# Query weight sums begun in the attention, MLP copies moved to w_xo's panels, a fourth raw buffer and two bank copies moved ahead on ScalarE

## The chip, the core and the metric

The kernel runs on one core of one Trainium2 chip. The metric is the device time of one execution in microseconds (us). Shorter is better. The engines are named as the profile names them: PE is TensorE, DVE is VectorE, ACT is ScalarE, POOL is GpSimd and SP is SyncE, which here only issues DMAs.

## The reference, cut to what matters

One layer of a streaming encoder: 512 tokens, width 1024, float32 in and out.

```python
hn = rmsnorm(h, norm_mix_g)
proj = hn @ w_in        # fox q,k,v,f | hgrn q,f,i,g
fox_out = fox_attention(...)         # 8 heads of 64, causal, forgetting bias
rec = hgrn2_chunkwise(...)           # 4 heads, state 128x128, gated recurrence
h = h + concat([fox_out, rec]) @ w_out
h = h + memory_cross_attention(rmsnorm(h, norm_x_g), mem_n, w_xq, w_xkv, w_xo)
u = rmsnorm(h, norm_ff_g) @ w1
h = h + square(relu(u)) @ w2
return rmsnorm(h, final_norm_g)

def memory_cross_attention(h, mem_n, w_q, w_kv, w_o):
    q = h @ w_q                      # 4 heads of 256; the queries of this text
    k, v = split(mem_n @ w_kv)
    p = softmax(q k^T / 16)
    return (p v) @ w_o
```

## The kernel before

**Arithmetic.** Every float32 product is made of three passes over tensors that are split into a rounded part (hi, "h") and a remainder (lo, "l"): hi x hi, hi x lo and lo x hi. A weight therefore passes through four steps: a DMA brings a raw block of 128 x 1024 values (0.5 MB) into a raw buffer, ACT copies it into a hi tile (line 189), DVE subtracts to get the lo tile (line 193), and PE uses both. Four hi and four lo tiles exist (`whp`, `wlp`), so a split waits until PE has left an earlier unit.

**Seven products for eight.** Several large products are done as 2 x 2 blocks with seven block products in the place of eight. Each needs combinations of blocks. Products are named 1 to 7; numbers 1, 2 and 3 take a weight block as it stands, 5, 7, 6 and 4 take sums of blocks. Part of the input projection, the queries (`w_xq`), the MLP's `w1` ("u", up) and `w2` ("d", down) are done in this way. For the queries there are two groups g = 0 and 1, hence 14 products, called 01, 11, 02 and so on in the order `QORDER`:

```python
QORDER = "01 11 02 05 06 07 04 03 15 12 16 17 14 13"
```

The sums over weight blocks are made in DRAM by DMAs. For each set (q, u or d, and a group) the function `sum_jobs` (line 535) first copies three blocks from DRAM to DRAM on SP's queue (line 542, "copies"; tiles `wsq`, `wsu`, `wsd`), and then POOL issues three accumulating DMAs on these copies (line 552, "sums"). There are 17 sets: two for the queries, seven for up, eight for down, so 51 copies and 51 sums. Sum number 4 of the queries and the MLP is made in SBUF: the raw tile of product 6 is kept, and POOL adds one more block to it (line 326) after the split for product 6 has read it. Product 4 then splits the same tile.

**When copies are issued.** The copies wait in the list `copies`. They are taken from it when weight panels are loaded (`load_unit`, line 199): each half panel takes as many as the table `COPIES` gives for the number of panels so far. Panel numbers: 12 to 18 are the last of w_in and first of the memory values, 19 and 20 the second memory values, 21 to 24 the memory keys, 25 to 28 w_out, 29 to 42 the 14 query units, 43 to 46 w_xo. Eight copies come earlier (`product_unit`). `q_unit` (line 302) takes one more for each query unit. The first loads of the MLP (`add_first`) take a copy each for four parts, and a sum whose copy has not been made by then fetches it.

**When sums are issued.** `Presum` (line 556) counts `spent`, the time of the matmuls that call `tick`, at 2400 columns per us. From the first value of the table `PACE` on, a sum is issued each time `spent` has grown by the gap that PACE gives for that stretch. The sum waits for the matmul at which it was due. Sets are taken in turn, two at a time: all six of the queries first, then u1 and d0, u2 and d1, and so on.

**Order around the change.** PE's order is written out by hand (`manual_schedule`): chunked recurrence, then 16 steps of attention with filler work between them (second value half, the third and fourth q/k pair, memory values, memory keys), then w_out (`residual`, "wo"), then the first seven query products back to back (`q_product`, line 1459, called for `QORDER[:7]`), then cross attention with the other seven as filler, w_xo ("xw"), and the MLP. ACT, DVE, POOL and SP are ordered by a list scheduler by priority, which is the order in the program, shifted by `ahead(n)`: positive n moves an instruction forward. Splits in `next_panel` have `PW` = -20. `P1` is 20. The order is fixed at build time, and each engine then runs in order. A tile pool hands out its buffers as that scheduler frees them.

**The query products.** Products of one group share PSUM banks U, V and Y. Product 1 fills U; V is started with a copy of U (line 1464) when product 2 comes; product 6 goes on in U, which is then copied to Y (line 1483); product 7 goes on in U after that copy has read it. Product 5 starts Y and its result is copied out (line 1481). The inputs 5, 6, 7 and 3 are sums of blocks of x (`x1_sums`, line 1413: DVE steps at line 1421, hi on ACT at 1425, lo on DVE at 1427 and 1429), written after the last residual sum of w_out (line 1362). Raw buffers of query units: two tiles of `wrp` and the one of `t4p` in turn, and for product 6 a tile of the pool `s4` (12 tiles), which also holds hT (4), the memory values (4) and the differences `xdif`, `xdif7`.

**w_xo and the MLP.** Raw buffers for w_xo come from `wrp` and `t4p`; the MLP has five in turn, and product 6 and the closing tiles come from `s4`.

Of the kernel before, what the change touches and what calls it, by code (L numbers as in the profile page):

```python
# [12 lines left out]
AF = mybir.ActivationFunctionType  # L13
# [6 lines left out]
D = 1024  # L20
# [12 lines left out]
P1, P2, P3, P4, PW = 20, 20, 20, 10, -20  # L33
# [6 lines left out]
NEG = -3.0e38  # L40
SEVEN = (1, 2, 3, 4, 5, 6, 7)
RAWS, HB, LOADS = 5, 4, 8
COPIES = {12: 2, 19: 1, 20: 0, 24: 1}
PACE = (150.0, 4.7), (301.0, 11.5)


@with_exitstack
def emit(
# [22 lines left out]
    te, ve, ac, gp = nc.tensor, nc.vector, nc.scalar, nc.gpsimd  # L71
# [26 lines left out]
    def s4(shape, name, dt=F32):  # L98
        return s4p.tile([P] + shape, dt, tag="s4", name=name)
# [7 lines left out]
    def t4(name):  # L107
        return t4p.tile([P, D], F32, tag="t4", name=name)

    def t2(name, dt=F32, shape=(S,)):  # L110
        return t2p.tile([P] + list(shape), dt, tag="t2", name=name)
# [6 lines left out]
    def mm(name, shape=(S,)):  # L118
        return mmp.tile([P] + list(shape), F32, tag="mm", name=name)
# [4 lines left out]
    def sc(name, shape=(S,)):  # L124
        return scp.tile([P] + list(shape), F32, tag="sc", name=name)
# [49 lines left out]
    state = {"used": 0, "halves": 0}  # L175
    copies, copied = deque(), set()
    UW, UK = WT + FH, KC // 2

    def new_parts(shape, name):
        pad = [P, UK * (UW + FH)]  # L180
        hi = whp.tile([P, shape[0] * shape[1]], R, tag="wh", name=f"wh{name}", padded_shape=pad)
        lo = wlp.tile([P, shape[0] * shape[1]], R, tag="wl", name=f"wl{name}", padded_shape=pad)
        return [t.rearrange("p (k n) -> p k n", k=shape[0]) for t in (hi, lo)]

    def split_of(hi, lo, raw):
        def split(what="hl"):
            at = None
            if "h" in what:
                at = ac.activation(hi, raw, AF.Copy)  # L189
            if "v" in what:  # L190
                ve.tensor_copy(hi, raw)
            if "l" in what:
                at_lo = ve.tensor_tensor(lo, raw, f(hi), ALU.subtract)  # L193
                return at or at_lo
            return at

        return split

    def load_unit(name, spec, ks, parts=1, between=None):
# [12 lines left out]
        for q in range(parts):  # L212
# [5 lines left out]
            if between is not None:  # L218
                between(q)
            for _ in range(next((n for at, n in reversed(COPIES.items()) if len(stream) >= at), 0)):  # L220
                if copies:
# [80 lines left out]
    def q_unit(g, name):  # L302
        hi, lo = new_parts([UK, WT], f"q{g}{name}")
        stream.append(([hi], [lo]))
        if name == "4":
            raw = q_raw.pop(g)
        else:
            if name == "6":
                raw = q_raw[g] = s4([UK, WT], f"wrq{g}{name}")
            else:  # L310
                state["halves"] += 1
                if state["halves"] % 3 == 0:
                    raw = t4(f"wrq{g}{name}")
                else:
                    raw = wrp.tile([P, D], F32, tag="wr", name=f"wrq{g}{name}", padded_shape=[P, UK * UW])
                raw = raw.rearrange("p (k n) -> p k n", k=UK)
            if name in SUMS:
                src = wsum["q", g, name]
            else:
                src = block_q(g, {"1": "00", "2": "10", "3": "11"}[name])  # L320
            nc.sync.dma_start(raw, src)
        if copies:
            tc.keep_in_program_order(copies.popleft()())
        jobs = [split_of(hi, lo, raw)]
        if name == "6":
            jobs.append(lambda: tc.keep_in_program_order(gp.dma_start(raw, block_q(g, "10"), accum_op=ALU.add)))
        return jobs
# [60 lines left out]
    def ahead(n):  # L388

        return tc.high_priority(offset=n) if n else nullcontext()  # L390

    class Fill:
        def __init__(self):
            self.q = deque()
            self.credit = 0.0
# [132 lines left out]
    def block_q(g, rc):  # L528
        r, c = int(rc[0]), int(rc[1])
        n0 = g * HG + c * WT  # L530
        return w_xq[r * S : (r + 1) * S, n0 : n0 + WT].rearrange("(k p) n -> p k n", p=P)
# [24 lines left out]
    class Presum:  # L556
        def __init__(self):
            self.jobs, self.spent, self.next, self.at = deque(), 0.0, PACE[0][0], None

        def emit(self):  # L560
            while self.jobs:
# [5 lines left out]
                tc.add_manual_dep(dma.ins, self.at.ins.name, sync, reason="presum")  # L567
                if self.spent >= PACE[-1][0]:
                    tc.keep_in_program_order(dma)
# [4 lines left out]
        def tick(self, us, at):  # L574
            self.spent, self.at = self.spent + us, at
            while self.jobs and self.spent >= self.next:
                gap = next(gap for begin, gap in reversed(PACE) if self.next >= begin)
                if gap is None:
                    self.next = min(begin for begin, _ in PACE if begin > self.next)
                    continue  # L580
# [205 lines left out]
    for hp in range(2):  # L786
# [8 lines left out]
        for j in range(2):  # L795
            h = 2 * hp + j
            ps = mm(f"gq{h}")
# [52 lines left out]
    U, W = [], []  # L850
# [112 lines left out]
    for li, m in enumerate(mlev):  # L963
# [10 lines left out]
        for hp in range(2):  # L974
# [3 lines left out]
            ps = sc(f"lv{hp}{m}", (NT, 2, w))  # L978
# [465 lines left out]
    qbank, y5s = {}, {}  # L1444
# [14 lines left out]
    def q_product(g, name):  # L1459
        b = {"5": "Y", "3": "Y", "2": "V"}.get(name, "U")  # L1460
        if (g, b) not in qbank:
            qbank[g, b] = (pvt if (g, b) == (0, "Y") else mm)(f"xq{b}{g}").rearrange("p (i n) -> p i n", i=2)
            if b == "V":
                ac.activation(qbank[g, b], qbank[g, "U"], AF.Copy)
        ps = qbank[g, b]
        (whi,), (wlo,) = next_panel()
        xh, xl = x1s[name]
        for k in range(UK):
            for i in range(2):
                ws, begin = slice(i * P, (i + 1) * P), name in "15" and k == 0 and i == 0  # L1470
                te.matmul(ps[:, i, :], whi[:, k, ws], xh[:, k, :], start=begin, stop=False, skip_group_check=True)
                te.matmul(ps[:, i, :], whi[:, k, ws], xl[:, k, :], start=False, stop=False, skip_group_check=True)
                at = te.matmul(ps[:, i, :], wlo[:, k, ws], xh[:, k, :], start=False, stop=k == UK - 1, skip_group_check=True)
            yield presum.tick(6 * WT / 2400, at)
        if name == "2":
            q_out(2 * g, 0, ps, 1.0)
        elif name == "4":
            q_out(2 * g, 1, ps, 1.0)
        elif name == "5":
            y5s[g] = t2(f"xy5{g}", F32, (2, M))  # L1480
            ac.activation(y5s[g], ps, AF.Copy)
        elif name == "6":
            ac.activation(qbank[g, "Y"], ps, AF.Copy)
        elif name in "73":
            t = t2(f"xt{name}{g}", F32, (2, M))
            ve.tensor_tensor(t, ps, y5s[g], ALU.add)
            q_out(2 * g + 1, 1 if name == "7" else 0, t, -1.0)

    for g, name in QORDER[:3]:
        run_now(q_product(g, name))  # L1490
# [4 lines left out]
    for g, name in QORDER[3:QN]:  # L1495
        run_now(q_product(g, name))
# [685 lines left out]
```

## Time and profile before

| | |
|---|---|
| median of 3 runs | 762.55 us (762.04 to 767.69) |
| the profiled execution | 764.74 us |
| its span, first to last instruction | 763.0 us |
| mean granted PE clock | 0.989 |
| PE busy | 742.7 us, 97% of the span |
| PE weight load (PEld) busy | 653.8 us, 86% |
| DVE busy | 585.3 us, 77% |
| ACT busy | 475.3 us, 62% |
| POOL busy | 221.2 us, 29% |
| moved by DMA | 168.68 MB |

The profile is of one execution. Its times start at the first instruction of the span; the 1.7 us between span and execution time lie around it. A row of a timeline gives start, duration, engine, line, operation, tile written and tiles read, and in brackets how long the engine was idle before and who released it. A row of the waits gives engine, tile and line that waited, then who it waited for, with us in total, times, and the longest. A row of a stage gives its length, busy us (with the number of instructions) of PE, PEld, DVE, ACT and POOL, the granted PE clock, the DMA share (mean busy share of the 16 DMA engines; it can pass 1 where packets overlap) and GB/s. A row of DMA issues gives tile and source, queue, count, size and median us from issue to landing. A matmul's duration is modelled with its pipeline; the distance between starts shows the rate.

### The profile page before, as it was taken

What the parts mean: (1) busy time and instruction counts of PE and PEld (TensorE: products, weight loads), DVE (VectorE), ACT (ScalarE), POOL (GpSimd) and SP (SyncE); (2) the same over time, 40 slices, a digit from 0 to 9 for tenths busy, and PEclk for the clock granted to TensorE, in tenths of its full rate; (3) what the DMA queues carried; (4) which work ended last, traced back from release to release, by engine and by line L of the source; (5) the groups of instructions that cost most, each with busy time, mean ns of one, the idle gap of its engine ahead of it and who ended that gap; (6) DMA issues with size and microseconds to landing.
All of it is one profiled execution on the core that took longest, in us unless ns stands there. A gap on an engine that the chain in (4) does not pass through costs nothing.

```text
span 763.0 us, 12700 instructions
## 1 busy us (share of the span) xinstructions
PE 742.7 (97%) x4701; PEld 653.8 (86%) x4701; DVE 585.3 (77%) x923; ACT 475.3 (62%) x792; POOL 221.2 (29%) x298
## 2 busy tenths in 40 slices
PE   9999999999999999869999999999999999999996
PEld 6888888898888888769887899898999999998985
DVE  5876996687788855956656699978878787969696
ACT  5865876576566632535445479758575757584864
POOL 7225942431453356422111212111111111110024
PEclk9999999999999999889999999999999999999999
DMA  8796999758969999988656799898998989797452
GB/s 249 225 222 192 262 293 351 226 181 267 326 180 258 319 293 281 217 190 160 141 142 117 159 224 241 227 245 225 238 219 239 230 221 244 212 244 208 151 111 110
DMA packets 118608, 168.68 MB, mean 221 GB/s; under 512 B 6625, under 2 KB 79626, under 8 KB 118546
## 3 DMA queue, kind: packets, MB, share of 16 engines
q1 hardware_dynamic: 88466, 119.87, 47.7%
q0 software_dynamic: 29920, 47.74, 35.3%
q8 instruction: 37, 0.61, 0.3%
q10 hardware_dynamic: 160, 0.27, 0.1%
q14 instruction: 25, 0.20, 0.1%
HBM read 162.59 MB, written 57.69 MB: 289 GB/s over the span
## 4 chain that ended last, share of the span: by engine, by line
PE 77%; DMA 9%; DVE 7%; ACT 4%; issue 2%; POOL 0%; SPq 0%; POOLq 0%; DVEq 0%; ACTq 0%
PE uU L1757 4%; PE uU L1759 4%; PE uU L1758 4%; DMA wrq<-in_w_xq_dram 3%; PE U L1916 3%; PE U L1915 3%; PE U L1917 3%; PE uY L1759 2%; PE uY L1758 2%; PE uY L1757 2%; PE xk L1189 2%; DMA wr28b<-in_w_out_dram 2%; PE xw L354 2%; PE xw L355 2%; PE Y L1916 2%
## 5 line engine op out<-in xcount | busy, mean ns | idle before, releaser
L193 DVE TENSOR_TENSOR wlu<-wru,whu 128x1024 fp32r<-128x1024 f32 x53 | 63.9, 1220 | 28.4 <-ACT whu L189 28.4
L189 ACT ACTIVATE whu<-wru 128x1024 fp32r<-128x1024 f32 x53 | 55.8, 1058 | 44.1 <-PE U L1917 16.8
L193 DVE TENSOR_TENSOR wld<-wrd,whd 128x1024 fp32r<-128x1024 f32 x56 | 68.2, 1221 | 13.3 <-ACT whd L189 12.9
L189 ACT ACTIVATE whd<-wrd 128x1024 fp32r<-128x1024 f32 x56 | 58.9, 1052 | 12.0 <-PE uU L1758 5.7
L1915 PE MATMUL U<-whd,hb 128*128 128x512 f32 x120 | 46.8, 390 | 0.0
L1916 PE MATMUL U<-wld,hb 128*128 128x512 f32 x120 | 46.8, 390 | 0.0
L1917 PE MATMUL U<-whd,hb 128*128 128x512 f32 x120 | 46.7, 389 | 0.0
L552 POOL DMA_DIRECT2D wsu<-in_w_dram x14 | 16.5, 1182 | 81.7 <-PE xw L355 22.6
L1757 PE MATMUL uU<-xs_hi,whu 128*128 128x256 f32 x128 | 36.3, 284 | 0.0
L1759 PE MATMUL uU<-x_hi,wlu 128*128 128x256 f32 x128 | 36.2, 283 | 0.0
L1757 PE MATMUL uY<-xs_hi,whu 128*128 128x256 f32 x128 | 36.2, 283 | 0.0
L1758 PE MATMUL uY<-xs_lo,whu 128*128 128x256 f32 x128 | 36.2, 283 | 0.0
L1759 PE MATMUL uY<-xs_hi,wlu 128*128 128x256 f32 x128 | 36.2, 283 | 0.0
L1758 PE MATMUL uU<-x_lo,whu 128*128 128x256 f32 x128 | 36.2, 283 | 0.0
L1758 PE MATMUL uU<-xs_lo,whu 128*128 128x256 f32 x128 | 36.2, 283 | 0.0
L1759 PE MATMUL uU<-xs_hi,wlu 128*128 128x256 f32 x128 | 36.2, 283 | 0.0
L1757 PE MATMUL uU<-x_hi,whu 128*128 128x256 f32 x128 | 36.2, 283 | 0.0
L1653 POOL DMA_DIRECT2D wru<-in_w_dram x7 | 9.2, 1314 | 85.2 <-DVE wlu L193 85.2
L552 POOL DMA_DIRECT2D wsd<-in_w_dram x16 | 17.9, 1122 | 53.8 <-PE xw L355 15.7
L1210 POOL TENSOR_SCALAR bi<-nF,Ft 128x128 f32<-128x128 f32 (+3 forms) x32 | 20.5, 649 | 43.4 <-PE pt L1246 20.4
L189 ACT ACTIVATE whq<-wrq 128x1024 fp32r<-128x1024 f32 x14 | 14.5, 1052 | 24.3 <-DMA wrq<-in_w_xq_dram 15.2
L193 DVE TENSOR_TENSOR wlq<-wrq,whq 128x1024 fp32r<-128x1024 f32 x14 | 17.0, 1221 | 15.9 <-ACT whq L189 15.9
(994 smaller groups left out, 2768.3 us busy)
## 6 DMA issues: line engine op xcount, KB each, us to landing
wru<-in_w_dram SPq DMA_DIRECT2D x25, 512.0 KB, 7.2
wsd<-in_w_dram SPq DMA_DIRECT2D x24, 512.0 KB, 6.9
wrd<-in_w_dram SPq DMA_DIRECT2D x24, 512.0 KB, 4.5
wrd<-wsd SPq DMA_DIRECT2D x24, 512.0 KB, 6.8
wsu<-in_w_dram SPq DMA_DIRECT2D x21, 512.0 KB, 7.5
wru<-wsu SPq DMA_DIRECT2D x21, 512.0 KB, 7.1
wsd<-in_w_dram POOLq DMA_DIRECT2D x16, 512.0 KB, 8.4
wsu<-in_w_dram POOLq DMA_DIRECT2D x14, 512.0 KB, 7.4
```

The costliest lines, as they stand in the source:

```text
L189: at = ac.activation(hi, raw, AF.Copy)
L193: at_lo = ve.tensor_tensor(lo, raw, f(hi), ALU.subtract)
L354: te.matmul(ps, wh, lo, start=False, stop=False)
L355: at = te.matmul(ps, wl, hi, start=False, stop=k == order[-1])
L552: yield gp.dma_start(wsum[kind, g, name], src, accum_op=ALU.add, **more)
L1210: gp.tensor_scalar(bi[:, 0:n], fF[h][:, 0:n], -1.0, Ft[:, tb, h : h + 1], op0=ALU.mult, op1=ALU.add)
L1757: te.matmul(ps[:, i, :], whi[:, k, ws], xh[:, k, :], start=begin, stop=False, skip_group_check=True)
L1758: te.matmul(ps[:, i, :], whi[:, k, ws], xl[:, k, :], start=False, stop=False, skip_group_check=True)
L1759: at = te.matmul(ps[:, i, :], wlo[:, k, ws], xh[:, k, :], start=False, stop=k == UK - 1, skip_group_check=True)
L1915: te.matmul(ps, hi, whi[:, k, :], start=begin, stop=False, skip_group_check=True)
L1916: te.matmul(ps, hi, wlo[:, k, :], start=False, stop=False, skip_group_check=True)
L1917: at = te.matmul(ps, lo, whi[:, k, :], start=False, stop=k == 1, skip_group_check=True)
```

## The change

Five things are altered.

- `COPIES`: from panel 20 to 42 no copies are taken (before: one per half panel from 24); from panel 43 (w_xo) one per half panel.
- `PACE`: five stretches. The first sum comes at spent 107 and not at 150; gaps are 6, then 5.5 from 143, 11.5 from 195, 6 from 240, and 9.5 from 301. Before: 4.7 from 150 and 11.5 from 301.
- `q_unit` takes no copy.
- `q_unit` has a fourth raw buffer, a tile of `s4`, and the tiles are taken in a turn of four.
- the copies U to V and U to Y on ACT are moved forward by `ahead(P1)`.

```diff
-COPIES = {12: 2, 19: 1, 20: 0, 24: 1}
-PACE = (150.0, 4.7), (301.0, 11.5)
+COPIES = {12: 2, 19: 1, 20: 0, 43: 1}
+PACE = (107.0, 6.0), (143.0, 5.5), (195.0, 11.5), (240.0, 6.0), (301.0, 9.5)
@@ def q_unit
                 state["halves"] += 1
-                if state["halves"] % 3 == 0:
+                if state["halves"] % 4 == 0:
                     raw = t4(f"wrq{g}{name}")
+                elif state["halves"] % 4 == 2:
+                    raw = s4([D], f"wrq{g}{name}")
                 else:
                     raw = wrp.tile([P, D], F32, tag="wr", name=f"wrq{g}{name}", padded_shape=[P, UK * UW])
...
             nc.sync.dma_start(raw, src)
-        if copies:
-            tc.keep_in_program_order(copies.popleft()())
         jobs = [split_of(hi, lo, raw)]
@@ def q_product
             if b == "V":
-                ac.activation(qbank[g, b], qbank[g, "U"], AF.Copy)
+                with ahead(P1):
+                    ac.activation(qbank[g, b], qbank[g, "U"], AF.Copy)
...
         elif name == "6":
-            ac.activation(qbank[g, "Y"], ps, AF.Copy)
+            with ahead(P1):
+                ac.activation(qbank[g, "Y"], ps, AF.Copy)
```

## The prediction, as put on record before the changed kernel ran

> **What bounds the kernel now.** I read the page first, then the waits of TensorE, then the busy times by stage.
>
> ```profile
> span 763.0 us, 12700 instructions
> ...
> PE   9999999999999999869999999999999999999996
> ...
> PEclk9999999999999999889999999999999999999999
> ...
> PE xqU L1471 <- ACT xqY L1483: 4.9, 1, 4.9
> PE xqV L1471 <- ACT xqV L1464: 3.8, 1, 3.8
> PE xqU L1471 <- DVE xt L1486: 2.2, 2, 1.4
> ```
>
> Each digit is one fortieth of the span. TensorE is busy nearly everywhere, so a change can pay only where it is not: at the end, which the diff does not touch, and in slices 17 and 18 (305 to 343 us), where the granted clock dips too. The three waits name the place: the query products.
>
> ```profile
> 155.40:169.60 14.20, 14.20 (x120) 14.20 (x120) 11.19 (x33) 10.79 (x26) 4.29 (x8) 1.00 0.64 223
> 169.60:185.30 15.70, 15.70 (x92) 13.12 (x92) 11.61 (x28) 8.86 (x19) 4.24 (x11) 1.00 0.71 240
> 185.30:200.00 14.70, 14.70 (x92) 12.21 (x91) 12.37 (x32) 11.28 (x25) 6.70 (x12) 1.00 1.01 310
> 200.00:217.20 17.20, 17.20 (x117) 14.19 (x116) 13.46 (x31) 9.84 (x19) 4.75 (x12) 1.00 0.55 202
> ...
> 232.20:263.30 31.10, 31.10 (x214) 27.06 (x212) 25.82 (x64) 21.70 (x47) 10.38 (x17) 1.00 1.07 287
> 265.30:309.00 43.70, 43.70 (x194) 36.15 (x193) 25.25 (x28) 13.17 (x19) 22.82 (x19) 1.00 1.11 289
> 309.00:344.70 35.70, 26.20 (x177) 25.57 (x176) 26.10 (x32) 16.48 (x22) 12.84 (x13) 0.81 0.84 190
> ```
>
> After the stage come its length, the busy time of PE, PEld, DVE, ACT and POOL, then clock, DMA share and GB/s. Four stages are attention with its filler, the fifth the same with the key projections, the sixth is w_out, the seventh the first seven query products. DMA stands at its ceiling (1.07 to 1.11) for 77 us ahead of the query stage, and there TensorE loses 9.5 us of 35.7, with the clock at 0.81.
>
> How the loss arises is read from ACT and DVE:
>
> ```profile
> 305.22 1.06 ACT L189 ACTIVATE whq<-wrq 128x1024 fp32r<-128x1024 f32 x1 [7.92 <-DMA wrq<-in_w_xq_dram]
> ...
> 316.19 1.99 ACT L189 ACTIVATE whq<-wrq 128x1024 fp32r<-128x1024 f32 x2
> 318.08 0.57 ACT L1464 ACTIVATE xqV<-xqU 128x512 f32<-128x512 f32 x1
> ...
> 333.05 2.00 ACT L189 ACTIVATE whq<-wrq 128x1024 fp32r<-128x1024 f32 x2 [3.70 <-DMA wrq<-in_w_xq_dram]
> 334.96 0.58 ACT L1483 ACTIVATE xqY<-xqU 128x512 f32<-128x512 f32 x1
> ...
> 306.31 1.23 DVE L193 TENSOR_TENSOR wlq<-wrq,whq 128x1024 fp32r<-128x1024 f32 x1 [5.75 <-ACT whq L189]
> ...
> 313.49 0.68 DVE L1362 TENSOR_TENSOR hT<-hT,wo 128x512 f32<-128x512 f32 x1
> ...
> 323.66 1.21 DVE L193 TENSOR_TENSOR wlq<-wrq,whq 128x1024 fp32r<-128x1024 f32 x1
> ```
>
> A late load holds ACT for 7.92 us, DVE behind it for 5.75, and the last residual sum, whose product was done at 309.0, runs only at 313.49. The two copies from bank to bank stand behind weight splits in ACT's order, the second behind one that itself waits 3.70 us for a transfer.
>
> **The change part by part.**
>
> ```profile
> 309.02 0.28 PE L1471 MATMUL xqU<-x_hi,whq 128*128 128x256 f32 x1
> ...
> 314.65 0.28 PE L1473 MATMUL xqU<-x_hi,wlq 128*128 128x256 f32 x1
> 318.70 0.58 PE L1471 MATMUL xqV<-x_hi,whq 128*128 128x256 f32 x1 [3.77 <-ACT xqV L1464]
> ...
> 335.59 0.58 PE L1471 MATMUL xqU<-o_hi,whq 128*128 128x256 f32 x1 [4.94 <-ACT xqY L1483]
> ...
> 318.60:323.80 5.20, 5.09 (x24) 0.52 0.81 116
> ...
> 335.50:341.00 5.50, 5.38 (x24) 0.53 0.55 157
> ```
>
> *The ceiling.* The first 48 matmuls (products 01 and 11) go from 309.02 to 314.77, 0.120 us each, so a product of 24 takes 2.88 us. Five more follow by 344.7 (02, 05, 06, 07, 04) and a row-sum step of 0.8: 15.2 us, an end at 330.0. At most 14.7 us are to be had: the gaps of 3.77 and 4.94, the two half-clock products after them (5.1 and 5.4 instead of 2.88), and 1.3 in small gaps. The half clock goes with its gap, since only the two long gaps are followed by one. The Trainium skill, "TensorE: Matmul & The Clock Gate", Part 1, says that an idle window of about 3.4 us halves the clock; the 3.77 and 4.94 agree, and by it any remaining gap under 3.4 us would cost only itself.
>
> *The DMA load.* "Spent" in PACE counts ticked matmul time. Summed over the code it stands at 106.6 where the second value half starts (155.4 us), 147.5 at the second memory-value product, 178.2 at w_out, 219.2 at 309.0. The first sum's value of 150 lands in the first row here, as it should:
>
> ```profile
> 220.53 1.23 POOL L552 DMA_DIRECT2D wsq<-in_w_xq_dram  x1 [1.35 <-PE xv L383]
> ...
> L542 SPq DMA_DIRECT2D wsd<-in_w_dram x24: 547/700/4545, 90.2 to 295.2; - x24
> ...
> wsd<-in_w_dram SPq DMA_DIRECT2D x8, 512.0 KB
> wsu<-in_w_dram SPq DMA_DIRECT2D x5, 512.0 KB
> ...
> q1 hardware_dynamic: 88466, 119.87, 47.7%
> q0 software_dynamic: 29920, 47.74, 35.3%
> ```
>
> The two SP rows in the middle are those of 236 to 300 us: 13 copies, all of which move out of the stage (8 to w_xo's panels, 4 to the MLP's first loads, 1 later). The queue shares price a 0.524 MB transfer: 47.7% of 763 us over 119.87 MB is 1.6 us of all engines for one from SP, and 35.3% over 47.74 MB is 3.0 us for one of POOL's sums. By the new PACE the sums per stage become 2, 2, 2, 1 in the four stages from 155.4 (none before), 4 from 232.2 (as before), 5 from 265.3 (8 before), 2 from 309.0 (5 before). So 232 to 263 loses seven copies, 11 of 33 us of DMA work, and falls to about 0.7; 265 to 309 loses six copies and three sums, 18.5 of 48.5, and falls to 0.7. What remains are loads of this size:
>
> ```profile
> wrd<-in_w_dram SPq DMA_DIRECT2D x24, 512.0 KB, 4.5
> ...
> wrq<-in_w_xq_dram SPq DMA_DIRECT2D x6, 512.0 KB, 11.8
> ...
> wrq<-in_w_xq_dram POOLq DMA_DIRECT2D x2, 512.0 KB, 6.9
> ...
> 360.00:380.00 20.00, 18.49 (x137) 17.36 (x136) 12.93 (x24) 10.55 (x20) 1.96 (x2) 1.00 0.64 138
> ...
> 447.00:640.00 193.00, 193.00 (x1311) 179.78 (x1310) 160.92 (x197) 134.33 (x187) 30.40 (x29) 1.00 0.93 237
> ```
>
> I take 4.5 us for a load where 11.8 stood (bounds: these two), the row of a stage at 0.93 that never stalls. With the fourth raw buffer the loads start ahead of the split before them, so product 11's split can come when its buffer is free, as w_out's last panel begins, 48 of the stage's matmuls (43.7 / 194 = 0.225 us) before 309.0: 298 instead of 305, and the last residual sum at 309.9 instead of 313.5. The buffer comes from the pool of 12 tiles that also holds hT, the memory values and the difference tiles; I count 12 in use at most, so no wait, bounded by one load (4.5).
>
> *The copies on ACT.* U into V moves ahead of splits and stands ready at about 312.5, before its use at 314.8. U into Y reads what product 06 ends with, and 07 overwrites it, so its own 0.58 and the signalling stay: 0.8, by the wait on xt (2.2 in two, one of them 1.4). What they pass, splits, has the slack given below.
>
> *What is late next.* DVE needs 324.87 - 313.49 = 11.4 us from the last residual sum to the end of 06's split; from 309.9 that is 321.3. The low half of 05's split is two 1.2 us operations earlier, 318.9, against a need at 318.5 or a little after; 06 is needed at 321.4. So DVE just keeps up, 0 to 1 us lost. Then 04: its weights are 06's raw tile plus a transfer that POOL issues after 06's split (325.41 before), 321.5 + 1.0 + 6.9 = 329.4, then ACT 1.1: 330.5. TensorE reaches 04 at 314.8 + 4 x 2.88 + 0.8 + 0.8 + 0.8 (xt) = 328.7, so 1.8 is lost; the lower bound is 0, if the transfer lands in 5. The end comes at 328.7 + 1.8 + 2.9 = 333.4 with all of it, 331.6 with none. I take 333: 11.7 us sooner than 344.7.
>
> *Early sums.* From 155.4 to 217.2 the four rows hold 44.7 us of DMA work; seven sums add 21, so 65.4 over 61.8 us, a share of 1.06, below the 1.11 under which w_out's 43.7 us ran without a gap. The densest stage, 185 to 200, would need 20.8 us of work where 14.7 x 1.11 = 16.3 fit: loads up to 4.5 us late. The slack is larger:
>
> ```profile
> 194.95 1.23 DVE L193 TENSOR_TENSOR wl18b<-wr18b,wh18b 128x1024 fp32r<-128x1024 f32 x1 [0.27 <-ACT wh18b L189]
> ...
> 205.26 0.39 PE L353 MATMUL pq<-hn_hi,wh18b 128*128 128x512 f32 x1
> ```
>
> The weights are ready 9.1 us before TensorE wants them. Cost nothing, hidden by that lead; 4.5 if the lead were used up. POOL's bias steps stand behind a waiting sum at most until its matmul, as they did from 220 on, without a gap on TensorE.
>
> *The MLP's sums and copies.* From 304 spent a sum comes every 9.5 instead of 11.5: some three more sums in 447 to 640, 9 us in 193, so 0.93 becomes 0.98. Of the copies twelve, 12 x 1.6 = 19 us of DMA work, go between 343 and 447, where the new gap of 6 instead of 4.7 lets some four sums (12 us) fewer run and a stage stands at 0.64. Nothing, up to 2 us.
>
> The sum: 764.74 (the profiled run; span 763.0) - 11.7 = 753.0. The median of the runs shown, 762.55, is 2.2 lower, so the forecast for the median is 750.9, said as 751.
>
> **The rivals.**
>
> *DVE's chain stays.* If only the two copies help and the residual sum does not come sooner (the order on ACT and DVE still has a blocked split ahead), 05 starts at the end of its split, 322.6, 06 at 325.5, 07 at 329.2, and 04's transfer, issued at 325.4 as now, gives 04 at about 335.5 to 338.4: gain 6, a median of 756.5. For it: DVE is busy from 312 to 328. Against it: its idle 5.75 came from DMA.
>
> *The change does not empty the stage.* Loads hoisted early, or the in-order SP queue waiting for a tile of the 12-tile pool, put the late load back: one wait of 4 to 8 us with its 2.3 us of half clock remains at each of two products; gain 0 to 2, median 761.5.
>
> *Slower: early sums crowd the attention.* Sixteen sums now run without a break from 155 to 281 us, and if accumulating transfers slow the loads beside them more than their share says, the 9 us lead is gone and each split holds ACT, with the softmax steps behind it. It decides once a half panel lands over 9 us later than now. The price, by the 3.70 us that a split waited for a transfer: six halves x 3.7 = 22, with 11.7 gained elsewhere, +10.5, a median of 773. For it: 185 to 200 is at 1.01 already. Against it: 232 to 309 at 1.07 to 1.11 with sums at the same spacing and no gap. The Trainium skill, "DMA: Bandwidth & Descriptors", section "Issuing engines are not separate DMA queues", speaks for it: transfers from SP and POOL interleave on the same 16 engines, so moving a sum earlier moves its contention with it; no row here shows sums beside this attention stage's copies.
>
> **How the numbers follow.** Forecast 0.70 (748 to 754), DVE's chain 0.13, not emptied 0.07, slower 0.10. A measurement of this kernel can tell about 1%, 7.6 us, from no change. Faster by over 1% is below 754.9: the forecast and a quarter of the second case, 0.74. Within 1%: the rest of it, the third, and a mild form of the fourth, 0.18. Slower: 0.08. The range starts at 762.55 - 14.7 - 1 = 747 (all of the ceiling, and a small later gap) and reaches to 760, which takes in the second case and part of the third; the slower case stays out.
>
> **What would show it.** Right: the waits on xqV L1464 and xqY L1483 below 1 us; DMA share near 0.7 from 232 to 309; no row of ACT waiting for wrq by over 2 us before 320; clock 1.00 throughout 309 to 333; 04's product waiting for its summed tile by up to 2 us; no gap between 155 and 309. Wrong: gaps on TensorE in 155 to 300 put down to ACT or DMA; SP waiting on the difference tiles; DVE's residual sum still near 313.

## The result, and the profile after

The changed kernel takes 773.5 us (median of 6 runs, 770.72 to 775.63) where the kernel before takes 763.73 (6 runs). The ratio is 1.0123, with a 95% interval of 1.0093 to 1.0154: slower by 1.2%. The forecast was 751, faster.

The page after, its span and the rows of TensorE and of the clock in 40 slices:

```profile
span 771.9 us, 12694 instructions
...
PE   8799999999888999979999999999999999999996
...
PEclk9999999999999999989999999999999999999999
```

TensorE now dips in three places and not in one: in the second slice, in slices 11 to 13, and in slice 18 (the query products). The waits of TensorE after (who waits, for whom, us in total, times, longest) name them:

```profile
PE pt L1246 <- DVE bi L1234: 6.1, 3, 2.6
PE gf L353 <- ACT hn_hi L609: 4.5, 1, 4.5
PE xqU L1472 <- ACT xqY L1485: 4.3, 1, 4.3
PE xqU L1472 <- DVE xt L1488: 1.6, 2, 0.8
```

The first is a transpose of softmax rows in the attention, the second the gate projection at the start, and neither wait stood in the kernel before. Of the query products' two long waits, the one for xqV is gone and the one for xqY stays (4.9 before).

The table below cuts each profiled execution at the first matmul of four stages. All later runs are in it too. Each entry is rounded on its own, so a row can differ from its span by 0.1.

| us | to the first value product | attention and w_out | query products | cross attention and w_xo | MLP to the end | span |
|---|---|---|---|---|---|---|
| before | 155.4 | 153.6 | 35.7 | 97.3 | 321.0 | 763.0 |
| after | 161.3 | 163.1 | 28.9 | 96.3 | 322.3 | 771.9 |
| e1, copies pinned | 155.4 | 162.0 | 28.1 | 96.3 | 322.6 | 764.3 |
| e2, sums as before | 162.1 | 153.6 | 30.6 | 98.2 | 321.0 | 765.5 |
| e3, copy before split | 160.6 | 160.9 | 25.1 | 96.3 | 322.4 | 765.4 |
| e4, sums alone | 155.2 | 160.8 | 28.9 | 97.0 | 322.3 | 764.3 |
| e5, three repairs | 155.1 | 153.6 | 27.1 | 96.6 | 321.7 | 754.1 |
| e6, small sums | 155.7 | 154.3 | 29.8 | 97.0 | 322.6 | 759.4 |
| e7, plain copies | 155.3 | 155.1 | 29.2 | 97.0 | 322.7 | 759.3 |
| e8, no copies beside | 155.5 | 154.1 | 30.2 | 98.5 | 321.7 | 759.9 |
| e9, gaps alone | 155.8 | 156.4 | 29.0 | 97.0 | 321.0 | 759.3 |
| e10, gaps and order | 155.6 | 154.6 | 24.1 | 97.0 | 323.5 | 754.8 |
| e11, copies alone | 155.0 | 153.6 | 31.5 | 97.3 | 321.0 | 758.4 |
| e12, all and order | 153.8 | 153.6 | 25.5 | 96.2 | 322.0 | 751.1 |

From before to after the stages change by +5.9, +9.5, -6.8, -1.0 and +1.3, together +8.9, the difference of the spans. The query stage, where the whole gain was forecast, did gain; the start and the attention, both costed at nothing, together lost over twice as much.

**The start.** SP's queue after, from 11 us on (start, duration, line, what is written from what):

```profile
11.53 1.97 SPq L542 DMA_DIRECT2D wsd<-in_w_dram  x2
13.73 0.43 SPq L215 DMA_DIRECT2D wr1a<-in_w_in_dram  x1
14.21 1.21 SPq L542 DMA_DIRECT2D wsd<-in_w_dram  x2
15.63 0.97 SPq L215 DMA_DIRECT2D wr1b<-in_w_in_dram  x1
```

Four copies for the MLP's last down products run between the first weight loads. In the kernel before, wr1a was issued at 11.58 and no copy ran before 78.24. ScalarE after:

```profile
23.16 1.06 ACT L189 ACTIVATE wh1a<-wr1a 128x1024 fp32r<-128x1024 f32 x1 [4.99 <-DMA wr1a<-in_w_in_dram]
24.12 0.67 ACT L609 ACTIVATE hn_hi<-xn,g_mix 128x512 fp32r<-128x512 f32 x1
```

The split waits 4.99 us for wr1a, and hn_hi, which does not read wr1a, stands behind it. TensorE waits 4.5 us for hn_hi.

**The attention.** Stages after, cut at the starts of the attention's filler products (length, busy us and instructions of PE, PEld, DVE, ACT and POOL, clock, DMA share, GB/s); the last two are w_out and the query products:

```profile
161.30:175.80 14.50, 14.47 (x120) 14.27 (x120) 11.29 (x34) 10.86 (x26) 7.92 (x12) 1.00 0.83 216
175.80:191.50 15.70, 15.70 (x92) 13.09 (x91) 11.98 (x27) 8.88 (x19) 6.94 (x13) 1.00 1.11 301
191.50:209.00 17.50, 14.86 (x92) 12.13 (x91) 10.27 (x28) 8.87 (x20) 5.59 (x11) 1.00 1.10 305
209.00:230.40 21.40, 17.86 (x118) 14.14 (x117) 13.88 (x34) 10.90 (x23) 9.65 (x15) 1.00 0.86 245
...
280.80:324.40 43.60, 43.60 (x193) 36.10 (x193) 31.72 (x30) 14.73 (x21) 24.72 (x18) 1.00 0.80 200
324.40:353.40 29.00, 23.95 (x178) 23.45 (x177) 22.00 (x29) 15.13 (x20) 7.65 (x8) 0.88 0.68 152
```

The second and third stage stand at a DMA share of 1.11 and 1.10, where before they had 0.71 and 1.01; from the third on TensorE is idle (17.50 less 14.86, 21.40 less 17.86). The first four rows are 7.3 us longer than their counterparts before (69.1 against 61.8); nearly all the rest of the 9.5 us lies in the stages left out, from 230.4 to 280.8 (50.4 against 48.1). ScalarE's splits in that stretch, then VectorE and TensorE at the first gap:

```profile
199.93 1.06 ACT L189 ACTIVATE wh18a<-wr18a 128x1024 fp32r<-128x1024 f32 x1 [3.96 <-DMA wr18a<-in_w_in_dram]
...
205.46 1.06 ACT L189 ACTIVATE wh18b<-wr18b 128x1024 fp32r<-128x1024 f32 x1 [1.70 <-DMA wr18b<-in_w_in_dram]
...
210.70 1.06 ACT L189 ACTIVATE wh19a<-wr19a 128x1024 fp32r<-128x1024 f32 x1 [1.27 <-DMA wr19a<-in_w_xkv_dram]
...
217.04 1.06 ACT L189 ACTIVATE wh19b<-wr19b 128x1024 fp32r<-128x1024 f32 x1 [3.71 <-DMA wr19b<-in_w_xkv_dram]
```

```profile
201.02 1.22 DVE L193 TENSOR_TENSOR wl18a<-wr18a,wh18a 128x1024 fp32r<-128x1024 f32 x1 [4.94 <-ACT wh18a L189]
...
203.88 0.60 DVE L1234 TENSOR_SCALAR bi<-bi,dn 128x256 f32<-128x256 f32 x2
```

```profile
204.36 0.63 PE L1246 MATMUL pt<-ident,bi 128*128 128x128 f32 x4 [2.64 <-DVE bi L1234]
```

A late load holds ScalarE, the low half holds VectorE for 4.94 us behind it, the softmax rows bi come after that, and TensorE waits for the rows. At this gap the weights themselves are not what TensorE waits for.

**The query products.** ScalarE after, and POOL's addition for unit 04:

```profile
342.51 1.06 ACT L189 ACTIVATE whq<-wrq 128x1024 fp32r<-128x1024 f32 x1 [3.82 <-DMA wrq<-in_w_xq_dram]
343.48 0.58 ACT L1485 ACTIVATE xqY<-xqU 128x512 f32<-128x512 f32 x1
```

```profile
336.58 1.33 POOL L326 DMA_DIRECT2D wrq<-in_w_xq_dram  x1 [7.30 <-issue]
```

The copy to bank Y still stands behind the split of unit 04, which waits for the tile that POOL began to add to at 336.58.

### The profile page after: what moved, and what is told of

It is laid out like the page before. It is cut to its first block, busy times and chain, and to the rows that moved or that the text cites. A ratio compares the mean times of both kernels' runs of the same rounds, so it can differ in the third digit from the quotient of the medians.

```text
span 771.9 us, 12694 instructions
## 1 busy us (share of the span) xinstructions
PE 743.0 (96%) x4701; PEld 651.9 (84%) x4701; DVE 588.7 (76%) x923; ACT 474.3 (61%) x792; POOL 227.6 (29%) x298
## 4 chain that ended last, share of the span: by engine, by line
PE 58%; issue 18%; DMA 8%; DVE 7%; ACT 5%; POOL 2%; SPq 0%; POOLq 0%; DVEq 0%; ACTq 0%
PE U L1917 3%; PE uU L1760 3%; PE uU L1759 3%; PE U L1918 3%; PE uU L1761 3%; PE U L1919 3%; PE wo L353 2%; PE wo L355 2%; PE wo L354 2%; PE xk L1189 2%; DMA wru<-in_w_dram 2%; DMA wr1b<-in_w_in_dram 2%; PE uY L1761 2%; PE uY L1759 1%; PE uY L1760 1%
## 5 line engine op out<-in xcount | busy, mean ns | idle before, releaser
L1655 POOL DMA_DIRECT2D wrd<-in_w_dram x8 | 9.7, 1218 | 85.3 <-DVE wld L193 85.3
L1210 POOL TENSOR_SCALAR bi<-nF,Ft 128x128 f32<-128x128 f32 (+3 forms) x32 | 24.8, 830 | 30.8 <-PE pt L1246 12.9
L1917 PEld LDWEIGHTS U<-whd,hb 128*128 128x128 f32 x120 | 22.5, 188 | 5.4 <-ACT hb L1864 0.5
```

The lines of the kernel that those rows point to most:

```text
L1210: gp.tensor_scalar(bi[:, 0:n], fF[h][:, 0:n], -1.0, Ft[:, tb, h : h + 1], op0=ALU.mult, op1=ALU.add)
L1655: tc.keep_in_program_order(gp.dma_start(box[0], block(g, "10"), accum_op=ALU.add))
L1917: te.matmul(ps, hi, whi[:, k, :], start=begin, stop=False, skip_group_check=True)
```

## The experiments

There are three losses and one gain. The theory was that each has a cause of its own: copies without a place in SP's order (start), sums beside copies (attention), the copy to bank Y behind a waiting split (query stage). Each repair was first tried alone.

**e1, copies pinned.**

```diff
-COPIES = {12: 2, 19: 1, 20: 0, 43: 1}
+COPIES = {12: 2, 19: 1, 20: 0, 43: 1, 45: 2}
```

> The changed kernel with one edit: from panel 45 on two copies per half panel are taken, so that all twelve late copies go with w_xo's loads and none is left for the MLP's first loads. Theory A (four copies that had no place of their own in SP's order ran at the very front and delayed the second gate weights): the weight loads wr1a and wr1b are first in SP's queue again, TensorE's wait on hn_hi of 4.5 us goes, the decay projection starts at 55.4 instead of 62.2, everything after is 6 us earlier and the time is 767.5 (766 to 769). Rival B (the start was late for another reason, such as a different order of pool tiles): the start stays at 62 and the time at 773.

764.83 us (10 runs, ratio 1.0014, 1.0000 to 1.0028). The first value product starts at 155.4 again and wr1a is issued at 11.91. The start is settled as A; the time is nearly 3 us below the expected one; attention and query stage came out about 1 us shorter each than in the changed kernel. In the program three of these copies are taken while the MLP's first product is written out and the fourth by a sum that finds its copy missing. There the order of SP is not held to an earlier SP instruction, and a copy from DRAM to DRAM waits for nothing, so the list scheduler could place it first. Why it did so is read from the code; the place itself is shown by the rows.

**e2, sums as before.** The changed kernel with the table of gaps of the kernel before.

```diff
-PACE = (107.0, 6.0), (143.0, 5.5), (195.0, 11.5), (240.0, 6.0), (301.0, 9.5)
+PACE = (150.0, 4.7), (301.0, 11.5)
```

> The changed kernel with the table of gaps of the kernel before, (150, 4.7) and (301, 11.5): the sums begin at the first memory keys again; everything else is as changed, the four copies at the front too. Theory A (the early sums, beside the copies and loads of the attention stage, cost the attention 9.5 us): from the first value product at 161.3 to the first query product it is 153.6 us again as before, not 163; query products start near 315 and the time is 773.5 - 9.5 = 764, less up to 3 given back in w_out or the query stage by denser sums. Rival B (the attention is longer because it starts later against loads that did not move, or because the fourth buffer or the copies moved tiles of the pool): the stretch stays 160 or more and the time stays above 770.

766.66 us (10 runs, 1.0024, 1.0008 to 1.0041). The attention is 153.6 to a tenth: A holds. The start stays at 162, as it must. The time is 2.7 above the expected 764, inside the 3 that was allowed for: 1.7 of it in the query stage, where POOL makes four sums again, and 2 in cross attention.

**e3, copy before split.**

```diff
+        if (g, name) == (0, "4"):
+            late4.append(jobs.pop())
...
-                ac.activation(qbank[g, "Y"], ps, AF.Copy)
+                copy_y = ac.activation(qbank[g, "Y"], ps, AF.Copy)
+            if g == 0:
+                split = late4.pop()()
+                tc.add_manual_dep(split.ins, copy_y.ins.name, order_only, reason="copy first")
```

> The changed kernel with the split of unit 04 kept behind the copy of bank U to bank Y on ScalarE; all else as changed. Theory A (the copy still stood behind that split, which waits for the summed tile): TensorE's wait of 4.3 us for xqY goes to under 1, the half clock after it goes too, product 04 then waits at most 1 us for its own split, the query stage is 5 to 6.5 us shorter (22.5 instead of 28.9) and the time is 768 (766.5 to 769). Rival B (the transfer of the summed tile is what sets the end of the stage, and the wait only moves from 07 to 04): the gap comes back ahead of 04 at 3 us or more, the stage is at most 2 us shorter, time 771.5 or more.

769.82 us (5 runs, 1.0068, 1.0047 to 1.0089): the gain was smaller than theory A's. The profiled execution is the fastest of the five (767.12). The gaps of TensorE in the query stage of e3:

```profile
337.71 0.39 PE L1474 MATMUL xqU<-o_hi,whq 128*128 128x256 f32 x1 [0.73 <-ACT xqY L1487]
343.72 0.36 PE L1474 MATMUL xqU<-x_hi,whq 128*128 128x256 f32 x1 [2.88 <-DVE xt L1494]
```

The wait for xqY falls from 4.3 to 0.73 and the half clock behind it goes, as A said. But 2.88 us come back ahead of product 04, as B said: the sum of product 07 (xt, line 1494 here) now stands on VectorE behind a low half that waits. The stage is 25.1, between the two theories.

**e4, sums alone.** The kernel before with the changed table of gaps and nothing else.

```diff
-PACE = (150.0, 4.7), (301.0, 11.5)
+PACE = (107.0, 6.0), (143.0, 5.5), (195.0, 11.5), (240.0, 6.0), (301.0, 9.5)
```

> The kernel before with one edit: the changed table of gaps (sums from 107 spent on). Copies as before, one for each half panel from 24 on, the query units too; three raw buffers. Theory A (sums in the attention stage alone make its loads late): the four waits of ScalarE for wr18a to wr19b of 1 to 4 us each appear, the stretch from the first value product to the first query product is 9 us longer (163 against 153.6), less what w_out gains by five sums instead of eight, which was not late before; time 763.7 + 9 = 772.5 (769 to 774). Rival B (the sums matter only together with the later start or the moved copies): the stretch stays within 2 us of 153.6 and the time within 761 to 766.

766.08 us (10 runs, 1.0020, 1.0005 to 1.0034). The attention is 160.8, so A holds for it: the sums do the harm without the later start and without the moved copies. What was not expected is the query stage: 28.9, exactly that of the whole change. The sums taken out of w_out and the query stage give the whole gain there, with the copies in place, three buffers, and both bank copies where they were. The longer attention could have given the loads this lead, but e6 to e8 below speak against that: with the same gaps and an attention within 1.5 us of before, their query stages take 29.2 to 30.2.

The loss could lie in POOL's queue (the bias rows of the softmax wait behind sums) or in the bytes. Three variants of e4 tell that apart.

**e6, small sums.**

```diff
-yield gp.dma_start(wsum[kind, g, name], src, accum_op=ALU.add, **more)
+rows_n = slice(0, 8 if early_n[0] < 8 else P)
+early_n[0] += 1
+yield gp.dma_start(wsum[kind, g, name][rows_n], src[rows_n], accum_op=ALU.add, **more)
```

> The kernel before with the changed table of gaps, as in the run of sums alone, but the first eight sums add only 8 of 128 rows (of 512 for the sums from the weights), so that the query weights of products 5, 6 and 7 lack most of their sum. POOL's queue, its waits and the order are those of sums alone; the bytes of the early sums are almost gone. Theory A (the transfers' bytes make the loads late): the stretch from first value product to first query product is 153.6 to 156 again. Rival B (the softmax's bias rows wait behind sums in POOL's queue): it stays near 160.8, the value with full sums.

**e7, plain copies.**

```diff
+early_n[0] += 1
+if early_n[0] <= 8:
+    yield gp.dma_start(wsum[kind, g, name], src, **more)
+else:
     yield gp.dma_start(wsum[kind, g, name], src, accum_op=ALU.add, **more)
```

> The kernel before with the changed table of gaps, but the first eight transfers of POOL copy their block and don't add it; the sums of the query weights are left out. Same bytes per transfer, same queue, same order. Theory A (a sum counts by the time it takes on the DMA engines, 3.0 us of all sixteen against 1.6 for a copy): about half of the 7.2 us of loss stays, the stretch is 156 to 158.5. Rival B (any POOL transfer of this size does the harm): 160 to 162. Rival C (only the adding does it): 154 to 155.

**e8, no copies beside.**

```diff
-COPIES = {12: 2, 19: 1, 20: 0, 24: 1}
+COPIES = {12: 2, 15: 0, 23: 1, 43: 2, 45: 3}
```

> The kernel before with the changed table of gaps, and the copies of panels 15 to 19 moved to the last key panels, w_out, the query units and w_xo, so that the early sums share the stretch from 150 to 210 us with weight loads alone. Theory A (sums and copies together overfill the DMA engines; either may stand alone): the stretch from first value product to first query product is 153.6 to 156. Rival B (sums delay the loads beside them whatever else runs): 159 or more.

The times are 761.07 us in e6 (4 runs), 760.96 in e7 (3 runs) and 761.74 in e8 (8 runs), where the kernel before took 764.12 beside them. The attention takes 154.3 in e6, 155.1 in e7 and 154.1 in e8, against 160.8 in e4 and 153.6 before. So e6 and e8 came out as their theories A say, and e7 lies nearest to its rival C. POOL's order is the same in e4, e6 and e7 but for a few neighbours that change places; in e6 and e7 POOL also spends less time on each issue, but in e8 it issues full sums as in e4, and the loss is gone there too. So it is the work of the transfers and not POOL's queue. Two stages of e4 follow, from the third q/k pair to the first memory values and the next, then the first of the two in e7 and in e8; the DMA share is last but one:

```profile
169.65:185.35 15.70, 15.70 (x93) 13.08 (x92) 11.62 (x27) 8.88 (x19) 6.62 (x13) 1.00 1.10 298
185.35:201.41 16.06, 14.82 (x92) 12.10 (x90) 11.00 (x31) 9.22 (x21) 6.53 (x11) 1.00 1.11 302
```

```profile
169.52:185.22 15.70, 15.70 (x93) 13.09 (x91) 11.61 (x27) 8.88 (x19) 5.62 (x13) 1.00 0.91 308
```

```profile
169.99:185.69 15.70, 15.70 (x93) 13.09 (x92) 11.62 (x27) 8.88 (x19) 6.61 (x13) 1.00 0.69 149
```

Either the adding or the copies beside it may be taken away; with both, two stages pass 1.0. The next stage stands at 1.01 in e7, as it did before (1.01), and TensorE is idle in neither. The halving that e7's theory A expected did not come: the loss is not in proportion to the work on the DMA engines. That a backlog of the first dense stage makes the second one late fits these rows, but no run shows it by itself.

The price of one transfer can be read from POOL's DMA queue in a stretch in which the bytes of one early transfer alone move (packets, MB, share of 16 engines), in e4 from 156 to 167.5 us and in e7 from 156 to 168 us:

```profile
q0 software_dynamic: 528, 0.52, 29.8%
```

```profile
q0 software_dynamic: 144, 0.52, 15.2%
```

The adding transfer takes 29.8% of 11.5 us, 3.4 us of all engines; the plain one 15.2% of 12 us, 1.8 us. GB/s alone would mislead here: in the stage above e7 moves more (308) at the lower share.

**e5, three repairs.** The changed kernel with e1's table of copies, new gaps, and e3's order, in which the low half of 04 is now kept behind the sum of product 07.

```diff
-COPIES = {12: 2, 19: 1, 20: 0, 43: 1}
-PACE = (107.0, 6.0), (143.0, 5.5), (195.0, 11.5), (240.0, 6.0), (301.0, 9.5)
+COPIES = {12: 2, 19: 1, 20: 0, 43: 1, 45: 2}
+PACE = (150.0, 4.7), (195.0, 11.5), (240.0, 4.7), (301.0, 9.5)
@@ def q_product, after the copy to bank Y
+                split = late4[0]("h")
@@ def q_product, after the sum of product 07
+                split = late4.pop()("l")
+                tc.add_manual_dep(split.ins, sum7.ins.name, order_only, reason="sum first")
```

> The changed kernel with three repairs: the late copies all in w_xo's panels (two per half panel from 45 on); sums from 150 spent on as before, at gaps 4.7, then 11.5 from 195, 4.7 from 240 and 9.5 from 301; and the split of unit 04 kept behind the copy to bank Y with its high half and behind the sum of product 07 with its low half. Theory A (the three losses are separate and add): decay projection at 55.4, the stretch from first value product to first query product 153.6, query stage 24.5 (25.2 with the copy alone in order, less about 1 for the sum of 07), cross attention as in the changed kernel (96 to 97), the MLP 1.3 longer than before: span 752.8, time 754.5 (752 to 757). Rival B (the sums not made in the attention come back as late transfers: ten sums in the key and w_out panels and the denser ones in cross attention make a load late): a gap of over 3 us in the query stage or w_xo, time 759 or more.

755.79 us (6 runs, 0.9894, 0.9877 to 0.9910): faster than both kernels, and within theory A's range. Start and attention are as A says; the query stage is 27.1 and not 24.5. TensorE there, in e5 (rows between are left out):

```profile
330.63 0.36 PE L1474 MATMUL xqU<-x_hi,whq 128*128 128x256 f32 x1 [2.65 <-DVE xt L1494]
330.82 0.28 PE L1475 MATMUL xqU<-x_lo,whq 128*128 128x256 f32 x1
331.67 0.39 PE L1476 MATMUL xqU<-x_hi,wlq 128*128 128x256 f32 x1 [0.57 <-DVE wlq L193]
...
332.83 0.41 PE L1475 MATMUL xqU<-x_lo,whq 128*128 128x256 f32 x1
333.04 0.41 PE L1476 MATMUL xqU<-x_hi,wlq 128*128 128x256 f32 x1
```

The wait for xt stayed: on VectorE the low half of the next unit, 15, now stood ahead of that sum and waited 2.72 us for its own high half. The last matmuls start 0.21 apart and not 0.12: the clock halved.

**e12, all and order, and e10, gaps and order.** e12 is e5 with the low half of 15 behind the sum too. e10 has the same order and the same gaps, but takes nothing else from the change: copies in w_out and the query units, three buffers, no copy moved forward with `ahead`.

```diff
+                late[1]("h")
+                for split in (late[0]("l"), late[1]("l")):
+                    tc.add_manual_dep(split.ins, sum7.ins.name, order_only, reason="sum first")
```

> The run with all three repairs, with the low half of unit 15 also kept behind the sum of product 07 (it stood ahead of that sum on VectorE and waited 2.72 us for its own high half). Theory A (TensorE's wait of 2.65 us for xt goes, and with it the half clock of the last 17 matmuls of product 04): query stage 27.1 - 2.0 - 1.5 = 23.6, and 04's low half is late by at most 1 us; time 752.5 (751.5 to 754). Rival B (VectorE is short of time: the low halves behind the sum make 04 or 03 wait as long): stage 26 or more, time 755 or more.

> The run of gaps alone plus the order around the query products: the split of unit 04 behind the copy to bank Y, and the low halves of 04 and 15 behind the sum of product 07. Copies stay in w_out and the query units, three raw buffers, bank V's copy where it was. Theory A (of the change only the wider gaps were worth anything; the moved copies, the fourth buffer and the copy forward on ScalarE gave nothing): query stage 24 to 25.5, time 753.5 (752 to 755), within 1 us of the run with the same order and the whole change. Rival B (they are needed once the order is right): a wait of 2 us or more for a load or for xqV comes back, stage 28 or more, time 757 or more.

e12: 753.02 us (4 runs, 0.9857, 0.9836 to 0.9879). e10: 753.20 us (6 runs, 0.9866, 0.9844 to 0.9888). They can't be told apart, so e10's theory A holds: with the right order, the moved copies, the fourth buffer and the V copy's move are worth nothing that shows beside intervals of about 1.6 us either way. e12's query stage missed its 23.6: TensorE's wait for xt went, but a half clock came back (last section). The longest waits of TensorE in e10's query stage are short:

```profile
PE xqU L1473 <- ACT whq L189: 0.9, 1, 0.9
PE xqU L1473 <- ACT xqY L1485: 0.7, 1, 0.7
PE xqU L1475 <- DVE wlq L193: 0.6, 1, 0.6
```

**e9, gaps alone, and e11, copies alone.** Each is the kernel before with one part: e9 the gaps of e5; e11 e1's table of copies and no copy in `q_unit`.

```diff
-PACE = (150.0, 4.7), (301.0, 11.5)
+PACE = (150.0, 4.7), (195.0, 11.5), (240.0, 4.7), (301.0, 9.5)
```

```diff
-COPIES = {12: 2, 19: 1, 20: 0, 24: 1}
+COPIES = {12: 2, 19: 1, 20: 0, 43: 1, 45: 2}
@@ def q_unit
-        if copies:
-            tc.keep_in_program_order(copies.popleft()())
```

> The kernel before with one edit, the table of gaps of the run with all three repairs: sums from 150 spent at 4.7, from 195 at 11.5, from 240 at 4.7, from 301 at 9.5. Copies, buffers and the order on ScalarE as before. Theory A (fewer sums in w_out and the query stage are enough to make the query loads early): attention 153.6 as before, query stage 29 to 31 instead of 35.7, the MLP 1.3 longer, time 758.5 (757 to 760). Rival B (the thirteen copies must go too): query stage 33 or more, time 762 or more.

> The kernel before with the copies alone moved: none from panel 20 to 42, one per half panel from 43 and two from 45, none in the query units. Sums, three buffers and the order as before. Theory A (copies out of w_out relieve the query loads as well as fewer sums do): query stage 30 to 31.5, as in the run with sums as before, time 759 (757.5 to 760.5). Rival B (there the fourth buffer and the copies forward on ScalarE did it): stage 34 or more, time 762 or more.

e9: 759.23 us (4 runs, 0.9939, 0.9915 to 0.9962), query stage 29.0. e11: 759.74 us (5 runs, 0.9943, 0.9924 to 0.9962), query stage 31.5. Both theories A hold for the time and the query stage; e9's attention (156.4) and MLP (321.0, no longer than before) are not as expected. Fewer sums shorten the query stage by 6.7 us, fewer copies by 4.2, and the two do not add: the whole change has 28.9. In both runs TensorE's wait for xqV is gone, so neither the fourth buffer nor `ahead` is needed for that, and the wait for xqY is what is left (5.2 in e9, 6.8 in e11).

## Why the prediction was wrong, step by step

**Early sums, costed at nothing: the step that failed.** The arithmetic of bandwidth in it was right. It worked out that the densest stage could not hold its transfers and that loads would come up to 4.5 us late; the longest waits of splits were 3.96 and 3.71. What failed was the cover, "hidden by that lead". The lead of 9.1 us is TensorE's, between the split of a weight and its use. The late load is met earlier, by the split on ScalarE and VectorE, and behind it stood softmax steps whose results TensorE wants at once. It cost 9.5 us (8.4 in e1, 7.2 in e4).

Nor were the rows of 1.07 to 1.11 before the query stage a proof that such a share is harmless. Between w_out's splits no softmax step stands. Between those of the key projections (232 to 263 us, 1.07) softmax steps do stand, but there the loads are issued earlier. Two loads of the kernel before with their splits (line, engine, count, ns of one, first and last start), one from the attention stage that lost, one from the key projections:

```profile
L215 SPq DMA_DIRECT2D wr18a<-in_w_in_dram x2: 373/440/507, 183.6 to 184.0; - x2
L189 ACT ACTIVATE wh18a<-wr18a x1: 1057/1057/1057, 189.8 to 189.8; 128x1024 fp32r<-128x1024 f32 x1
...
L215 SPq DMA_DIRECT2D wr25a<-in_w_out_dram x1: 487/487/487, 241.9 to 241.9; - x1
L189 ACT ACTIVATE wh25a<-wr25a x1: 1058/1058/1058, 252.9 to 252.9; 128x1024 fp32r<-128x1024 f32 x1
```

From issue to split, 18a to 19b have 5.3 to 6.2 us, and 24a to 26b 6.8 to 10.9. In the changed kernel 18a to 19b were split 8.4 to 9.8 us after issue, as soon as they had landed. A load that takes 8 to 10 us is late in the first place and hardly in the second, where no split waited over 0.95 us for a transfer. This is read from the rows; no run gave these loads an earlier issue.

**The moved copies, costed at nothing.** The step "4 to the MLP's first loads, 1 later" took the place in the program for the place in the queue. Four of these copies wait for nothing and were not tied to the queue's order; they were issued from 11.5 us on and cost 5.9 (e1). It was not among the rivals.

**The copy to bank Y, costed at 0.8.** Its wait stayed at 4.3 us with its half clock. The mechanism was misjudged: `ahead` changes a priority and not an order. That the scheduler took the split of 04 for ready first is read from the code; that the split stood first is shown by the rows. With the order tied, the copy costs 0.73, which is the size forecast (e3, e5, e10, e12). The query stage therefore gave 6.8 and not 11.7.

**What held.** The loads fell to 4.6 us against a forecast of 4.5, as the transfers of the w_out stage in the changed kernel show (a median):

```profile
wrq<-in_w_xq_dram SPq DMA_DIRECT2D x4, 512.0 KB, 4.6
```

The last residual sum came 0.2 us after its product, at 324.61, and 06's split ended 11.4 us later, as worked out; the wait for xqV went. The DMA share fell less than to the forecast 0.7: to 0.83 in the key projections (246.3 to 278.8 us) and 0.80 in w_out. The cause was credited too widely: e4 has all of this gain from the sums alone. With the three failed steps repaired (e12, whose early sums are gone altogether), 753.0 stands against the forecast of 751, a gain of 10.7 where 11.7 was summed up. The MLP's narrower gap of 9.5 costs 0 to 2.5 (321.0 to 323.5 over its runs, against 321.0 in all three at 11.5), within the 0 to 2 of the forecast but for one run.

**The rivals.** The slower one, early sums crowding the attention, named the mechanism that happened, and even its 773. That the number agrees is chance: six halves at 3.7 were to cost 22, against 11.7 gained, while 9.5 were lost there, 5.9 at the start and 1.3 in the MLP, and 7.8 gained. It was given 0.10 because w_out bore the same share without a gap; "DVE's chain stays" and "not emptied" did not occur.

## What to carry to other kernels

A lead counts for the engine that has it. Before a late load is called hidden, look at the first instruction that waits for it and at what is queued behind that instruction, not at the last consumer. A transfer that waits for nothing has no place of its own in a queue: when it is moved, tie it to a neighbour, and read the queue's order from its first row. And two reliefs of the same bottleneck need not add: try each alone before taking both.

## What the runs showed of the hardware that was not expected

The clock does not go by the length of a single gap. A gap of 2.88 us was followed by full speed (e3), while 2.65 and 0.57 with little work between were followed by half speed (e5). More plainly, e10 and e12 have the same three gaps at products 07 and 04 (0.73, 0.95 and 0.57 us in e12; 0.73, 0.94 and 0.57 in e10), and e12 ran most of 04 at half clock and e10 did not.

The traces show what differs. In each of the 14 traces the granted clock changes only at times that lie a whole number of 3.41 us apart. In the kernel before, for instance, it goes to half at 316.82, back at 323.64, to half at 333.88 and back at 340.71. One such step of e12 and the next, then one step of e10 and one of e3:

```profile
325.68:329.09 3.41, 1.90 (x14) 1.52 (x13) 2.27 (x3) 3.34 (x4) 0.39 (x2) 1.00 1.03 228
329.09:332.50 3.41, 3.41 (x18) 3.41 (x18) 2.43 (x3) 0.00 (x0) 0.00 (x0) 0.50 0.43 128
```

```profile
327.63:331.04 3.41, 2.37 (x18) 1.99 (x17) 1.41 (x2) 2.25 (x3) 1.22 (x2) 1.00 1.08 252
```

```profile
341.97:345.38 3.41, 1.66 (x14) 1.69 (x15) 3.33 (x4) 1.13 (x2) 0.00 (x0) 1.00 0.85 118
```

The gaps of 0.95 and 0.57 us fall into one step in e12, in which 12 matmuls of 256 columns start (3072 columns), and the next step runs at half clock. In e10 the gap of 0.57 lies mostly in the next step; 16 matmuls start in this one (4096 columns), and the clock stays full. In e3 the gap of 2.88 leaves room for 14 (3584 columns), and the clock stays full too. Over all 14 traces, a step at full clock in which matmuls of under 2816 columns started was always followed by half clock, and one with over 3072 never was; between the two both occur. This was found by counting in the traces afterwards; no run was made to test it.

The Trainium skill, "TensorE: Matmul & The Clock Gate", Part 1, puts the halving after an idle window of about 3.4 us. The gaps of 4.3 and more here agree with it, and those of e12, 2.25 us in all, do not; so short gaps close together have to be priced with the risk of a half-clock product, about 1.5 us here (25.5 in e12 against 24.1). Whether the risk comes true depends on where the gaps fall among the steps, and the steps of these traces lie differently in each execution.

An adding transfer costs the DMA engines about twice a plain one of the same size (3.4 against 1.8 us, e4 and e7). A DMA share just over 1 does not by itself say that TensorE will wait: two attention stages at 1.10 and 1.11 cost e4 7.2 us, while the kernel before ran 31.1 us of key projections at 1.07 and 43.7 us of w_out at 1.11 without a gap on TensorE in them.
